# One product for both halves of the input, with the two sums added on leaving PSUM, in the input projections of an encoder layer

## The chip, the cores and the metric

The kernel runs on one core of a Trainium2 chip. The metric is the device time of one execution in microseconds, the median of the runs.

## The reference, cut to what matters

One encoder layer on 256 tokens of width 1024, all in float32. A combined input projection of the normalised stream feeds eight heads of forgetting attention and eight heads of a gated linear recurrence (HGRN2), and gives sigmoid merge gates. Both branches are projected, gated, summed and projected once more; a layer norm follows, then a mixture of sixteen experts of which each token uses two.

```python
x = layer_norm(x, ln_in_g, ln_in_b)
h = x @ w_in[l] + b_in[l]
fq, fk, fv, ff, hq, hf, hi, hg, gates = split_cols(h, IN_SIZES)
...
f_gate = lb + (1.0 - lb) * jax.nn.sigmoid(z)          # z: heads of hf
q_h = jax.nn.silu(to_heads(hq, HGRN_HEADS))
...
g = jax.nn.sigmoid(gates)
mixed = (g[..., :D_MODEL] * y_fox + g[..., D_MODEL:] * y_hgrn) @ w_mix_out[l] + b_mix_out[l]
x = layer_norm(ALPHA * x + mixed, ln1_g[l], ln1_b[l])
y_moe = grouped_top2_moe(x, router_w, router_b, expert_w1[l], expert_w3[l], expert_w2[l])
```

## The kernel before, in words

Float32 precision is kept with products of a rounded type (fp32r): each operand is split into a high half (the value rounded) and a low half (what is left), and a product of two operands is made of three: high by high, high by low, low by high, all summed in PSUM.

The **front stage** does everything before the experts. Its weights come as 15 slots of 128 x 4096 floats, each cut into 8 units of 512 columns; `u` counts the units, 0 to 119. `KIND` says how a slot is multiplied. In a token-major slot ("tm": 0, 3, 6, 13, 14) the input is the stationary operand and 512 weight columns move. In a feature-major slot ("fm": 1, 2, 4, 5, 7 to 10) a weight block of 128 x 128 is stationary and the input moves, all 256 tokens; one output block of 128 features needs two units, and a slot has four blocks. Slots 11 and 12 ("f4") are feature-major too, with the outputs of the branches as the input. The eight "fm" slots are: 1 the forget gate of the recurrence (`ev_hf`), 2 its query (`ev_hq`), 4 the attention's query (`ev_q`), 5 its key (`ev_k`), 7 to 10 the merge gates (`ev_gate`).

`prep(u)` splits the weights of a unit: ACT casts them to the high half (three units have their cast on DVE), and DVE, or POOL for some units, subtracts to get the low half. High and low halves have four buffers each, so the halves of unit u can be made when the products of unit u - 4 are done. `mm(u)` issues the products of a unit, in a feature-major slot four steps of three products (L215, L216, L217). When a block is complete, its `evac` function takes it out of PSUM in the next round, with the bias and the gate's nonlinearity. PSUM tiles with the tag "g" have four banks.

The order on PE, ACT, DVE and POOL is written out by hand: each engine does its instructions in the order in which the program gives them. A round `i` of the main loop is: what `pe` has for the round; the split of unit 2i + 3; the products of unit 2i; the evacuation of the blocks that were complete; what `post` has for the round; the split of unit 2i + 4; what `mid` has; the products of unit 2i + 1. Through `post`, DVE gets the residual operations (`resid`, L337 to L344) in rounds 5 to 14, the small operations of the attention's forget gates (`f_log`, round 6, and `f_log2`, round 12), and from round 13 on the recurrence: `h_exps` and `h_mul` prepare its operands on DVE and ACT, `h_scores`, `h_mask` and `h_out` work them off, and `h_range1` to `h_range3` (rounds 20 and 21) look for the smallest decay, with a transpose on PE (L610) that waits for a reduction on DVE (L606). In round 12 `h_ln` takes logarithms on ACT, with a table load. Attention runs in rounds 29 to 40 beside the merge gates' slots.

The **expert stage** follows. Its weights (16 experts of three matrices) stream through buffers that the front stage and the experts before leave; all transfers are issued on one queue (SP), in a fixed order. An output of 256 x 1024 is written at the end.

Of the kernel before, what the change touches and what calls it, by code (L numbers as in the profile page):

```python
# [18 lines left out]
T, D, NE, S = 256, 1024, 16, 64  # L19
# [44 lines left out]
def trunk(ctx: ExitStack, tc: tile.TileContext, x, cst_d, rows_d, wf, we, lvl_d, out):  # L64
    nc = tc.nc
    V, A, G, PE = nc.vector, nc.scalar, nc.gpsimd, nc.tensor
# [22 lines left out]
    def bank(tag, shape, name=None):  # L89

        return ps.tile(shape, F32, name=name or tag, tag=tag, bufs={"g": 4, "s": 2, "o": 2}[tag])
# [27 lines left out]
    def C(name):  # L119
        a, b = _C[name]  # L120
        return cst[:, a:b]
# [42 lines left out]
    KIND = ["tm", "fm", "fm", "tm", "fm", "fm", "tm", "fm", "fm", "fm", "fm", "f4", "f4", "tm", "tm"]  # L164
# [20 lines left out]
    tmp = {}  # L185
    evac = {}
    done = []

    def mm(u, tts=(0, 1)):
        i, c = u // 8, u % 8  # L190
        hi, lo = split[u]
        rh, rl = operands[i]()
        if KIND[i] == "tm":
            for tt in tts:
                if c == 0:

                    tmp[tt] = ([(bank("g", [128, 256]), 0), (bank("o", [128, 256]), 256)] if i == 14 and tt == 1
                               else [(bank("g", [128, 512]), 0)])
                t = slice(tt * 128, (tt + 1) * 128)
                for p, a in tmp[tt]:  # L200
                    b = a + 512 // len(tmp[tt])
                    PE.matmul(p, rh(c)[:, t], hi[:, a:b], start=c == 0, stop=False, skip_group_check=True)  # L202
                    PE.matmul(p, rh(c)[:, t], lo[:, a:b], start=False, stop=False, skip_group_check=True)  # L203
                    PE.matmul(p, rl(c)[:, t], hi[:, a:b], start=False, stop=c == 7, skip_group_check=True)  # L204
                if c == 7:
                    done.append((i, tt, [p for p, _ in tmp[tt]]))
            return
        nk = 8 if KIND[i] == "fm" else 4
        k0 = 4 * (c % 2) if nk == 8 else 0
        if k0 == 0:  # L210
            tmp["p"] = bank("g", [128, T])
        p = tmp["p"]
        for kk in range(4):
            k, w = k0 + kk, slice(kk * 128, (kk + 1) * 128)
            PE.matmul(p, hi[:, w], rh(k), start=k == 0, stop=False)  # L215
            PE.matmul(p, hi[:, w], rl(k), start=False, stop=False)  # L216
            PE.matmul(p, lo[:, w], rh(k), start=False, stop=k == nk - 1)  # L217
        if k0 + 4 == nk:
            done.append((i, c // 2 if nk == 8 else c, p))


    def halves(name):

        t = [X.tile([128, 2, 2, T], F32R, name=name, tag="w", bufs=4) for _ in range(4)]
        return [lambda k, i=i: t[k // 2][:, i, k % 2, :] for i in range(2)], t

    xp, xt4 = halves("xp")
# [20 lines left out]
    def x_affine(tt, j):  # L248
        p = xq[tt, j]
        if j == 0:  # L250
            xq["t", tt] = P2.tile([128, 8, 128], F32, name="xt", tag="hk" if tt else "lf")
        xt = xq["t", tt][:, 2 * j:2 * j + 2, :]
        for i in range(2):
            k = slice(2 * j + i, 2 * j + i + 1)
            if j % 2 == 0:
                V.tensor_scalar(xt[:, i, :], p[:, i, :], C("ing")[:, k], C("inb")[:, k], op0=OP.mult, op1=OP.add)
            else:
                A.activation(xt[:, i, :], p[:, i, :], AF.Identity, bias=C("inb")[:, k], scale=C("ing")[:, k])
        xq[tt, j] = xt

    def x_hi(tt, j):
        A.copy(xt4[j][:, 0, :, tt * 128:(tt + 1) * 128], xq[tt, j])

    def x_lo(tt, j):
        t = slice(tt * 128, (tt + 1) * 128)
        (G if j == 3 or (tt, j) == (1, 1) else V).tensor_sub(xt4[j][:, 1, :, t], xq[tt, j],
                                                             xt4[j][:, 0, :, t].bitcast(F32))

    operands = {i: (lambda: xp) for i in range(11)}
    def x_parts(tt, j):  # L270
        x_affine(tt, j)
        x_hi(tt, j)
        x_lo(tt, j)
# [17 lines left out]
    prep(0)  # L291
    prep(1)
    mm(0, (0,))
    x_stats(1)
    V.bn_aggr(mvs(1), sm[:, 24:36])
    mm(1, (0,))
    A.activation(mvs(1)[:, 1:2], mvs(1)[:, 1:2], AF.Sqrt, bias=eps_in[:, 0:1])
    prep(2)
# [4 lines left out]
    x_turn(1, 0)  # L303
    x_turn(1, 1)
    mm(2, (0,))
    mm(3, (0,))
    x_affine(1, 0)
# [18 lines left out]
    mm(3, (1,))  # L326
    prep(5)
    x_parts(0, 3)
    prep(6)
    x_parts(1, 3)  # L330
    prep(7)

# [50 lines left out]
    def p4(dt=F32, shape=(128, 4, T)):  # L383
        return P1.tile(list(shape), dt, name="p4", tag="p4")

    hv = GP.tile([128, 2, 512], F32, name="hv")
    lf = P2.tile([128, 4, T], F32, name="lf")
    hk = P2.tile([128, 4, T], F32, name="hk")
    hqt = P2.tile([128, 4, T], F32, name="hqt")
    qT = p4()  # L390
    kT = p4()
    vt = PB.tile([128, 2, 512], F32, name="vt")
    late = {}
# [374 lines left out]
    def ev_gate(n):  # L768
        def ev(b, p):
            i = 4 * n + b  # L770
            A.activation(late["gates"][:, i, :], p, AF.Sigmoid if i >= NID else AF.Identity, bias=C("bg")[:, i:i + 1])
        return ev
# [83 lines left out]
                 13: lambda tt, p: (mix_add(0, tt, p), mix_stats(0, tt))})  # L856
    for n in range(4):
        evac[7 + n] = ev_gate(n)
    operands[11] = lambda: [lambda k, i=i: oH[i][:, k, :] for i in "hl"]
    operands[12] = lambda: [lambda k, i=i: oF[i][:, k, :] for i in "hl"]  # L860
    operands[13] = operands[14] = lambda: late["mp"]
# [389 lines left out]
    pm, w, s1, s2, n1 = [t16[:, i] for i in range(5)]  # L1251
# [52 lines left out]
    def gather(g):  # L1304
        p = bank("g", [128, 4, 128])
        for i in range(4):
            k = 4 * g + i
            for tt in range(2):
                PE.matmul(p[:, i, :], raw[:, tt, k * 128:(k + 1) * 128], oneh2[:, tt, :], start=tt == 0, stop=tt == 1)  # L1309
        return p  # L1310
# [34 lines left out]
    def turn_pe():  # L1345
        p = bank("g", [128, 4, 128])
        for i in range(4):
            PE.transpose(p[:, i, :], sg[:, i * 128:(i + 1) * 128], ident)  # L1348
        return p
# [180 lines left out]
    for e in range(0, NE, 2):  # L1530
# [25 lines left out]
        p = turn_pe()  # L1556
# [11 lines left out]
        if e < LAST:  # L1568
            p = gather(0)
# [3 lines left out]
        if e < LAST:  # L1573
            py[0], py[1] = [bank("g", [128, 512]) for _ in range(2)]
            down(e, 0)
            p = gather(1)
# [132 lines left out]
```

## Time and profile before

| | |
|---|---|
| median of 3 runs | 676.27 us (676.14 to 677.37) |
| the profiled execution, its own time | 677.44 us |
| its span, first to last instruction | 675.7 us |
| PE busy | 650.1 us (96%) |
| PE weight loads (PEld) busy | 386.8 us (57%) |
| DVE, ACT, POOL busy | 210.1, 195.6, 75.9 us |
| mean granted clock of PE | 0.988 |

Times are microseconds from the span's start. PE stands for the matmul engine, PEld for its weight loads, which overlap the products; DVE, ACT, POOL and SP are the vector, scalar, general and transfer-issuing engines. An engine counts as busy while an instruction of it is on record. Products are pipelined and their ends are modelled, so the pace of PE is read from start to start. L215 is line 215 of the kernel before. "[0.76 <-ACT hqt L407]" behind an instruction means that its engine sat idle for 0.76 us before it, until ACT's instruction of line 407 on the tile `hqt` had ended. A granted clock of 1.00 is 2.4 GHz, 0.50 is 1.2 GHz.

### The profile page before, as it was taken

The page shows a single profiled execution, that of the slowest core. Times are in us where ns is not written, and L with a number is a line of the kernel's source. Part 1 is how long each engine was busy: PE and PEld are TensorE (multiplying, and loading weights), DVE is VectorE, ACT ScalarE, POOL GpSimd, SP SyncE. Part 2 cuts the span into 40 slices and gives each one's busy share as a digit, 9 for nine tenths or more (in the row PEclk, how much of TensorE's full clock was granted, in tenths as well). Part 3 has the DMA queues.
Part 4 walks back from the last instruction along what each step waited for, and adds up shares of the span by engine and source line. Part 5 has one row for each costly group of instructions (what it writes and reads, how often), then busy time and mean ns, then how long its engine had stood idle before and what let it go on. Part 6 is the DMA issues. An engine that isn't in the chain of part 4 may idle for free.

```text
span 675.7 us, 9394 instructions
## 1 busy us (share of the span) xinstructions
PE 650.1 (96%) x3773; PEld 386.8 (57%) x3773; DVE 210.1 (31%) x472; ACT 195.6 (29%) x413; POOL 75.9 (11%) x74
## 2 busy tenths in 40 slices
PE   7999999999999999999999999959999999799996
PEld 7796998999998734435444533513443443343542
DVE  6788855554585511011011011000101101101014
ACT  4664466767455410121111111101011011001211
POOL 1203365232272000000000000000000000000001
PEclk8999999999999999999999999979999999989999
DMA  8959325636888799999999999999999999999992
GB/s 325 412 212 368 138 82 211 249 125 238 316 306 346 268 348 400 420 431 418 430 421 419 431 418 430 421 419 426 422 421 429 420 428 423 420 428 422 414 374 101
DMA packets 31444, 238.70 MB, mean 353 GB/s; under 512 B 3488, under 2 KB 3616, under 8 KB 20640
## 3 DMA queue, kind: packets, MB, share of 16 engines
q1 hardware_dynamic: 31248, 237.94, 86.7%
q8 instruction: 32, 0.52, 0.3%
q14 instruction: 20, 0.16, 0.1%
q10 hardware_dynamic: 144, 0.07, 0.0%
HBM read 236.95 MB, written 1.05 MB: 352 GB/s over the span
## 4 chain that ended last, share of the span: by engine, by line
PE 57%; DMA 23%; DVE 2%; POOL 1%; ACT 1%; issue 0%; DVEq 0%; ACTq 0%; SPq 0%; POOLq 0%
DMA w<-in_we_dram 23%; PE g L1340 21%; PE g L1357 9%; PE g L215 4%; PE g L216 3%; PE g L217 3%; PE g L1309 2%; PE g L1385 2%; PE acc L1374 1%; PE g L203 1%; PE g L1510 1%; PE g L204 1%; PE g L202 1%; PE g L1348 1%; PE g L1499 1%; PE g L1406 1%
## 5 line engine op out<-in xcount | busy, mean ns | idle before, releaser
L1340 PE MATMUL g<-w,e 128*64 128x512 f32 x992 | 223.0, 600 | 7.3 <-DMA w<-in_we_dram 7.3
L1340 PEld LDWEIGHTS g<-w,e 128*64 128x64 f32 x992 | 69.4, 138 | 139.5 <-issue 127.4
L1357 PE MATMUL g<-w,f 128*64 128x512 f32 x448 | 106.4, 604 | 2.9 <-DMA w<-in_we_dram 2.9
L182 DVE TENSOR_TENSOR lo<-w,hi 128x512 fp32r<-128x512 f32 x87 | 67.7, 789 | 49.3 <-ACT hi L181 48.4
L181 ACT CAST hi<-w 128x512 fp32r<-128x512 f32 x117 | 70.2, 618 | 38.9 <-PE g L216 31.5
L1357 PEld LDWEIGHTS g<-w,f 128*64 128x64 f32 x448 | 41.4, 138 | 57.5 <-issue 53.4
L215 PE MATMUL g<-xp,hi 128*128 128x256 f32 x256 | 74.3, 290 | 0.0
L217 PE MATMUL g<-xp,lo 128*128 128x256 f32 x256 | 72.5, 283 | 0.2 <-DVE lo L182 0.2
L216 PE MATMUL g<-xp,hi 128*128 128x256 f32 x256 | 72.4, 283 | 0.0
L182 POOL TENSOR_TENSOR lo<-w,hi 128x512 fp32r<-128x512 f32 x33 | 45.2, 1372 | 111.8 <-ACT hi L181 111.8
L1369 DVE SCALAR_TENSOR_TENSOR y<-g,sm,y 128x512 fp32r<-128x512 f32 x14 | 10.5, 751 | 142.5 <-ACT y L1368 142.5
L1619 POOL TENSOR_TENSOR e<-e,par 128x256 f32<-128x256 f32 x2 | 1.4, 726 | 448.9 <-ACT e L1618 448.9
L215 PEld LDWEIGHTS g<-xp,hi 128*128 128x128 f32 x256 | 48.9, 191 | 2.6 <-issue 1.4
L217 PEld LDWEIGHTS g<-xp,lo 128*128 128x128 f32 x256 | 49.0, 191 | 0.4 <-DVE lo L182 0.4
L216 PEld LDWEIGHTS g<-xp,hi 128*128 128x128 f32 x256 | 49.0, 191 | 0.0
L1309 PEld LDWEIGHTS g<-e,raw 128*128 128x128 f32 x224 | 26.1, 192 | 11.4 <-issue 11.4
L1320 ACT ACTIVATE e<-g,cst 128x128 f32<-128x128 f32 x28 | 10.5, 456 | 69.0 <-PE g L1309 69.0
L1563 DVE TENSOR_TENSOR e<-e,g 128x512 f32<-128x512 f32 x8 | 5.5, 687 | 76.2 <-ACT e L1562 76.2
L1309 PE MATMUL g<-e,raw 128*128 128x128 f32 x224 | 28.7, 282 | 0.0
L1368 ACT ACTIVATE y<-g,sm 128x512 fp32r<-128x512 f32 x14 | 9.6, 687 | 61.2 <-PE g L1357 28.4
L1572 ACT COPY f<-g 128x512 f32<-128x512 f32 x8 | 4.7, 585 | 69.6 <-PE g L1348 69.6
L1549 DVE TENSOR_TENSOR e<-e,g 128x512 f32<-128x512 f32 x8 | 5.5, 687 | 47.9 <-PE g L1340 47.9
(325 smaller groups left out, 756.9 us busy)
## 6 DMA issues: line engine op xcount, KB each, us to landing
w<-in_we_dram SPq DMA_DIRECT2D x70, 2048.0 KB, 24.6
w<-in_we_dram SPq DMA_DIRECT2D x94, 512.0 KB, 18.5
w<-in_wf_dram SPq DMA_DIRECT2D x13, 2048.0 KB, 8.8
w<-in_wf_dram SPq DMA_DIRECT2D x8, 512.0 KB, 9.5
w<-in_we_dram SPq DMA_DIRECT2D x16, 256.0 KB, 5.2
rbc<-in_rows_dram SPq DMA_DIRECT2D x1, 1036.0 KB, 13.6
f<-in_we_dram SPq DMA_DIRECT2D x4, 256.0 KB, 7.3
out_dram<-par SPq DMA_DIRECT2D x4, 256.0 KB, 2.1
```

Source lines behind the costliest of these rows:

```text
L181: A.copy(hi, src)
L182: (G if on_pool(u) else V).tensor_sub(lo, src, hi.bitcast(F32))
L215: PE.matmul(p, hi[:, w], rh(k), start=k == 0, stop=False)
L216: PE.matmul(p, hi[:, w], rl(k), start=False, stop=False)
L217: PE.matmul(p, lo[:, w], rh(k), start=False, stop=k == nk - 1)
L1309: PE.matmul(p[:, i, :], raw[:, tt, k * 128:(k + 1) * 128], oneh2[:, tt, :], start=tt == 0, stop=tt == 1)
L1320: A.activation(t[:, i, :], p[:, i, :], AF.Identity, bias=C("b1")[:, 4 + i:5 + i], scale=C("g1")[:, 4 + i:5 + i])
L1340: PE.matmul(h[64 * nh:64 * nh + 64, :], xg[kh][:, k, 64 * (e % 2):64 * (e % 2) + 64], wcol(e, m + kh, k, nh), start=kh + k == 0, stop=kh = ...
L1357: PE.matmul(py[nh][64 * a:64 * a + 64, :], hT[a][:, c0:c0 + 64], wt[:, nh * 512:nh * 512 + 512], start=f == 0, stop=f == 7)
L1368: A.activation(y["h"], py[nh], AF.Identity, scale=gs)
L1369: V.scalar_tensor_tensor(y["l"], py[nh], gs, y["h"].bitcast(F32), op0=OP.mult, op1=OP.subtract)
L1385: PE.matmul(W["y"][64 * a:64 * a + 64, :], hT[a][:, c0:c0 + 64], w[:, 0:q], start=f == 0, stop=f == 7)
```

## The change

In the "fm" slots the high half of a weight block meets the high and the low half of the input in one product: the input's halves lie in one tile (`xt4`), 256 columns of each are taken as 512 moving columns, and the sum goes to the two halves of a full PSUM bank. The product of the weights' low half with the input's high half is added to the first of them. A step thus has one product of 512 columns and one of 256. In the last step of a block the low half's product comes first. When the block leaves PSUM, ACT copies the second sum into the place where the block's result will lie, DVE adds it to the first in PSUM, and the evacuation goes on as before from the first. Slots 11 and 12 keep three products of 256, in a like order.

```diff
@@ -208,13 +208,22 @@
         nk = 8 if KIND[i] == "fm" else 4
         k0 = 4 * (c % 2) if nk == 8 else 0
         if k0 == 0:
-            tmp["p"] = bank("g", [128, T])
-        p = tmp["p"]
+            tmp["p"] = bank("g", [128, 2, T])
+        p, side = tmp["p"], i in both
         for kk in range(4):
             k, w = k0 + kk, slice(kk * 128, (kk + 1) * 128)
-            PE.matmul(p, hi[:, w], rh(k), start=k == 0, stop=False)
-            PE.matmul(p, hi[:, w], rl(k), start=False, stop=False)
-            PE.matmul(p, lo[:, w], rh(k), start=False, stop=k == nk - 1)
+            last = k == nk - 1
+            if side:
+
+                both_mm = lambda: PE.matmul(p, hi[:, w], both[i](k), start=k == 0, stop=last, skip_group_check=True)
+            else:
+                both_mm = lambda: [PE.matmul(p[:, 0, :], hi[:, w], r(k), start=k == 0 and r is rh, stop=last and r is rl,
+                                             skip_group_check=True) for r in (rh, rl)]
+            if not last:
+                both_mm()
+            PE.matmul(p[:, 0, :], lo[:, w], rh(k), start=False, stop=False, skip_group_check=True)
+            if last:
+                both_mm()
         if k0 + 4 == nk:
             done.append((i, c // 2 if nk == 8 else c, p))
 
@@ -267,6 +276,7 @@
                                                              xt4[j][:, 0, :, t].bitcast(F32))
 
     operands = {i: (lambda: xp) for i in range(11)}
+    both = {i: (lambda k: xt4[k // 2][:, :, k % 2, :]) for i in range(11)}
     def x_parts(tt, j):
         x_affine(tt, j)
         x_hi(tt, j)
@@ -856,6 +866,23 @@
                  13: lambda tt, p: (mix_add(0, tt, p), mix_stats(0, tt))})
     for n in range(4):
         evac[7 + n] = ev_gate(n)
+
+    home_of = {1: lambda b: lf[:, b, :], 2: lambda b: hqt[:, b, :], 4: lambda b: qT[:, b, :], 5: lambda b: kT[:, b, :]}
+
+    def side_by_side(i, fn, to):
+        def ev(b, p):
+            if i in both:
+                t = to(b)
+                A.copy(t, p[:, 1, :])
+                V.tensor_add(p[:, 0, :], p[:, 0, :], t)
+            fn(b, p[:, 0, :])
+        return ev
+
+    for n in range(4):
+        home_of[7 + n] = lambda b, n=n: late["gates"][:, 4 * n + b, :]
+    for n in range(13):
+        if KIND[n] != "tm":
+            evac[n] = side_by_side(n, evac[n], home_of.get(n))
     operands[11] = lambda: [lambda k, i=i: oH[i][:, k, :] for i in "hl"]
     operands[12] = lambda: [lambda k, i=i: oF[i][:, k, :] for i in "hl"]
     operands[13] = operands[14] = lambda: late["mp"]
```

## Rows read from the trace of the kernel before

**Rows 1.** Page: span, busy time of the engines, DMA share in 40 slices.

```profile
span 675.7 us, 9394 instructions
...
PE 650.1 (96%) x3773; PEld 386.8 (57%) x3773; DVE 210.1 (31%) x472; ACT 195.6 (29%) x413; POOL 75.9 (11%) x74
...
DMA  8959325636888799999999999999999999999992
```

**Rows 2.** Windows: length, busy us (count) PE, PEld, DVE, ACT, POOL; clock, DMA share, GB/s.

```profile
31.10:52.60 21.50, 21.50 (x175) 21.32 (x176) 18.11 (x39) 13.15 (x29) 1.64 (x2) 1.00 0.64 248
...
66.70:88.60 21.90, 21.27 (x190) 19.90 (x186) 17.98 (x54) 10.32 (x26) 7.03 (x5) 1.00 0.39 154
88.60:113.20 24.60, 24.45 (x165) 21.68 (x166) 11.06 (x17) 15.97 (x29) 13.89 (x11) 1.00 0.32 114
113.20:162.60 49.40, 49.40 (x419) 46.02 (x418) 28.59 (x92) 36.46 (x88) 17.75 (x17) 1.00 0.53 199
162.60:174.30 11.70, 11.70 (x101) 11.65 (x98) 4.93 (x8) 6.23 (x12) 2.57 (x2) 1.00 0.90 333
...
230.00:235.00 5.00, 5.00 (x37) 3.50 (x36) 0.73 (x2) 1.23 (x4) 0.00 (x0) 1.00 0.30 54
...
260.00:280.00 20.00, 20.00 (x106) 10.36 (x104) 2.07 (x3) 2.09 (x5) 0.00 (x0) 1.00 1.02 427
```

**Rows 3.** Timeline of PE: products three apart, of 512 and of 256 columns.

```profile
62.07 0.39 PE L202 MATMUL g<-hi,xp 128*128 128x512 f32 x1
...
62.76 0.39 PE L202 MATMUL g<-hi,xp 128*128 128x512 f32 x1
...
171.02 0.28 PE L215 MATMUL g<-xp,hi 128*128 128x256 f32 x1
...
171.38 0.28 PE L215 MATMUL g<-xp,hi 128*128 128x256 f32 x1
```

**Rows 4.** Timeline of ACT, DVE and PE around the end of slot 2.

```profile
45.80 0.62 ACT L181 CAST hi<-w 128x512 fp32r<-128x512 f32 x1 [0.82 <-PE g L216]
...
52.09 0.47 ACT L407 ACTIVATE hqt<-g,cst 128x256 f32<-128x256 f32 x1
...
52.59 0.48 DVE L408 SCALAR_TENSOR_TENSOR hqt<-g,cst,hqt 128x256 f32<-128x256 f32 x1 [0.76 <-ACT hqt L407]
...
55.35 0.17 DVE L692 TENSOR_TENSOR ff<-ff 128x16 f32<-128x16 f32 x1 [1.17 <-ACT ff L690]
...
58.03 0.50 PE L203 MATMUL g<-lo,xp 128*128 128x512 f32 x1 [0.69 <-DVE lo L182]
```

**Rows 5.** Lines by form: copy and add of 128x256 from PSUM, busy us, mean ns.

```profile
L715 ACT COPY nf<-g 128x256 f32<-128x256 f32 x4 | 1.5, 372 | 5.0 <-DVE nf L714 3.4 <-PE g L217 1.6
...
L782 DVE TENSOR_TENSOR gates<-g,gates 128x256 f32<-128x256 f32 x8 | 3.0, 416 | 0.0
```

**Rows 6.** Waits of DVE, 31.1 to 52.6 us: total us, times, longest.

```profile
DVE hqt L408 <- ACT hqt L407: 1.7, 2, 1.0
DVE lo L182 <- ACT hi L181: 1.4, 4, 0.5
```

**Rows 7.** Timeline of DVE and PE at the search for the smallest decay.

```profile
88.36 0.16 DVE L606 TENSOR_REDUCE hrg<-hrg 128x1 f32<-128x16 f32 x1
...
88.57 0.27 PE L610 MATMUL g<-cst,hrg 128*1 128x128 f32 x1 [0.63 <-DVE hrg L606]
```

**Rows 8.** Windows of line L217 alone: length, busy us (count) PE, PEld; clock, DMA.

```profile
88.60:101.00 12.40, 6.80 (x24) 4.59 (x24) 1.00 0.17 52
113.20:162.60 49.40, 27.10 (x96) 18.32 (x96) 1.00 0.53 199
162.60:174.30 11.70, 8.93 (x32) 6.14 (x32) 1.00 0.90 333
```

**Rows 9.** Windows around the longest wait of the expert stage, columns as in rows 2.

```profile
444.00:451.00 7.00, 0.57 (x5) 0.17 (x5) 0.00 (x0) 0.00 (x0) 0.00 (x0) 0.81 0.97 401
451.00:458.00 7.00, 7.00 (x24) 2.35 (x26) 0.00 (x0) 0.00 (x0) 0.00 (x0) 0.70 1.05 428
```

## Prediction

> **What bounds the kernel now.** I read the page first. PE is busy 96% of a span of 675.7 us and the DMA engines are full from about a third of the span on [rows 1], so one of the two sets the end everywhere. The windows by stage come next. From 260 us on, in the expert stage, the queues run without a pause; but at 230 to 235 us the DMA share is 0.30 [rows 2]: the transfers wait there for buffers that PE has not yet left. So whatever moves the moment at which the front stage (projections, attention, recurrence, mixing) ends moves the start of the saturated stretch by the same amount, and with it the end. The change lies wholly in the front stage, and I count front-stage time one to one.
>
> Inside the front stage PE is at its floor nearly everywhere (21.50 of 21.50, 49.40 of 49.40, 11.70 of 11.70 us busy [rows 2]). The floor itself is read from start to start, since ends are modelled: three products of 256 columns start 0.36 us apart in all, and three of 512 columns 0.69 us [rows 3], thus 0.120 and 0.230 us each. The weight load of the next product lies beside it.
>
> But two engines stand close behind PE. DVE is busy 18.11 of 21.50 us in the stretch of the first two feature-major slots and 17.98 of 21.90 us in the stretch of the recurrence [rows 2]. And at the seam between these stretches PE already waits for DVE: the product at 58.03 us starts late for a low half [rows 4], which means that there the weight halves are ready with no lead at all. Going back from it: the low half follows a cast on DVE, behind three small operations of which the first waited 1.17 us for a logarithm on ACT, behind the Ln table and the last sigmoid of slot 2 at 52.09 us [rows 4]. Elsewhere the halves come early: ACT's cast at 45.80 us waits for PE to leave a buffer [rows 4], with four buffers per half.
>
> **What the change removes.** In each of 256 steps (8 slots of 8 units of 4) the products of 256 columns go from three to one plus one of 512. One weight load goes too. The columns are the same, so only the per-product overhead is won: 0.360 before, 0.230 + 0.120 = 0.350 after, 0.010 us a step, if the doubled product with its two separate runs of 256 elements takes what a plain one takes (bounds: 0, if it costs two of 0.120; 0.013, if both shapes go at the best spacing in the traced stretches). All 256 steps give 2.6 us, and only where PE sets the pace.
>
> The Trainium skill speaks of the same saving: "TensorE: Matmul & The Clock Gate", section "Back-to-back issue gap", gives 262 cycles for 256 columns and 518 for 512, so the saving would be 6 cycles, 2.5 ns a step or 0.6 us in all. At 2.4 GHz 256 columns are 107 ns, so the rows show some 13 ns of overhead on a short product, more than the page has; the rows decide.
>
> **What it adds.** 32 blocks (8 slots of 4) each get a copy on ACT, priced by the nearest PSUM copy of the same shape at 372 ns, and an add on DVE, by a PSUM operation of the same shape at 416 ns [rows 5] (bounds 0.37, the copy's time, and 0.48, the PSUM operation at 52.59 us [rows 4]; no row writes PSUM from DVE). More weighs the order. Before, a block's first activation stands on ACT right behind the cast, and DVE comes to its result later. Now ACT copies, DVE adds behind the low half that precedes it in its queue, ACT's activation waits for the add, and DVE's next operation on the block waits for the activation. Behind the waiting activation stands the next weight cast; behind the waiting DVE operation stand a residual operation and the next low half.
>
> *Slots 1 and 2 (8 blocks, 31 to 52.6 us).* When DVE is the pacer, a block makes its chain longer by the add 0.42, the sigmoid 0.47, and two hand-offs of 0.03 (52.09 + 0.47 to 52.59 [rows 4]): 0.95 us. Eight make 7.6 us. DVE has 21.50 - 18.11 = 3.4 us idle there to set against it [rows 2]; 3.1 of that are waits on ACT's casts and sigmoids [rows 6], which vanish when DVE runs behind. One, about 0.2, stays, because a cast follows a sigmoid that itself waits for DVE. So the last sigmoid of slot 2, and with it the whole chain to the low half at 58 us, comes 7.6 - 3.4 + 0.2 = 4.4 us later. The lead of the halves (a cast can start when the unit four before is done, so some three units of 1.44 us less 1.3 us for cast and subtraction, 3.0 us) covers PE up to slot 2's end, but at 58 us the lead is nil, so PE takes the 4.4 us there in full. Bounds: 0 if the queues overlap so that only the adds' own 8 x 0.42 = 3.4 us count against the 3.4 idle; 5.5 if the add costs 0.48 and each block has a second hand-off.
>
> *Slot 4 (4 blocks, 66.7 to 88.6 us).* The stretch is a chain of DVE and ACT, and it ends where PE waits for the smallest decay, DVE's operation at 88.36 us [rows 7]. Four adds lie ahead of it: 4 x 0.42 = 1.7 us. The copies are hidden, as ACT has 10.32 of 21.90 us busy [rows 2]. The consumer of this slot is a DVE operation, so no hand-off back to ACT. Bounds 0 and 2.5 (each add also waits 0.2 for its copy).
>
> *Slots 5 and 7 to 10 (20 blocks).* Here PE is the pacer and ACT and DVE are 11 to 16 of 25 and 36 and 29 of 49 us busy [rows 2]. Twenty copies and stalls of ACT for the add (about 0.8 us each) fall into idle time; the halves lead by some 3 us, as above, so I cost them at nothing; without that cover up to 0.8 us for a block, some 3 us for the four blocks with a softmax round beside them. PE's gain counts in these: 24 + 96 + 32 = 152 steps [rows 8] x 0.010 = 1.5 us won (bounds 0 and 2.0).
>
> **The sum.** +4.4 + 1.7 - 1.5 = +4.6 us. The profiled execution took 677.44 us (span 675.7 and 1.7 around it), so 682.0; that execution lies 1.17 above the median of the runs shown, 676.27, so the forecast for the median is 680.9 us, 0.7% slower.
>
> **Rivals.** *A: DVE never becomes the pacer, and the change is faster.* If casts and adds interleave so that the eight blocks' lag at 52.6 us stays within idle time and the one at 88 us too, then all 256 steps count: 676.27 - 2.6 = 673.7 us. For it: the 3.0 us of lead and 3.4 us of idle. Against it: PE's wait at 58.03 us has no lead, and the order on each engine is fixed. It decides when the chain of eight blocks grows by under 0.43 us each (3.4 / 8). Chance 0.13.
>
> *B: partly absorbed.* Half of the lag (2.2) and half of slot 4 (0.8) against 2.0 won: +1.0, 677.3 us, within what can be told. Chance 0.10.
>
> *C: more is lost.* A stall of over 4 us at 58 us may bring the granted clock down: after PE's near idleness from 444 to 451 us (0.57 of 7.00 busy) it was 0.70 over the next seven [rows 9], so about 0.3 x 7 = 2.1 us of PE's work, and the softmax stretch may add 1 to 3. 684 to 686 us. Against it: PE has slack of waits behind 58 us anyway. Chance 0.08.
>
> *D: the doubled product takes twice 0.120*, so that nothing is won: +6.1, 682.4 us. It does then not do what it says. The plain product of 512 columns in rows 3 speaks against it. Chance 0.05.
>
> *E: the weight loads set PE's pace.* PEld is busy 11.65 of 11.70 us at 162.6 to 174.3 [rows 2]. If a load had to take its 0.120 us turn and the columns were free, two loads a step instead of three would save 256 x 0.120 = 31 us: 645 us. Against it: 512 columns start 0.230 apart with the same loads, so columns, not loads, pace. Chance 0.02. The rule behind it is the Trainium skill's "Perfetto Trace Analysis", section "Identifying the Most-Contended Engine": TensorE's headroom is judged by how busy LDWEIGHTS is. Here it misleads, as load records overlap their wait.
>
> **How the numbers follow.** The forecast itself has 0.62 (its own range 678.3 to 682.8). Slower by over 0.2% (1.35 us, about what a measurement of this kernel can tell from no change): forecast, C and D, 0.75. Within: B, 0.10. Faster: A and E, 0.15. The range leaves out most of A and E below and the upper part of C: 675.0 to 684.5 us.
>
> **What would show it.** Right: L217's partner of 512 columns 0.23 us from the next start; DVE's waits on casts gone between 31 and 52 us, and in their place DVE and ACT waiting for each other at the block's add and activation; the Ln table load some 4 us later than 52.58; PE's wait for the low half, now ending at 58.03, ending near 62; the wait for the decay at 88 us near 94; no new PE waits after 113; the first expert product about 4.6 us later, the expert stage as long as before. Wrong: if the Ln table load moves by under 1.5 us, the step of the eight blocks fails (A or B); if PE's steps do not shrink to 0.350, the removal fails (D); if new PE waits show at 120 to 160 us, "at nothing" fails (C); if the front is late but the end is not, the one-to-one step fails.

## The result, and the profile after

The changed kernel took 686.02 us (median of 4 runs, 684.32 to 686.96) against 676.62 us of the kernel before in the same session (4 runs, 676.14 to 677.37): a ratio of 1.0129, interval 1.0114 to 1.0144. The forecast of slower was right; the size was not: 9.4 us where 4.6 were forecast, and above the upper end of the range, 684.5. The profiled execution took 684.32 us, 6.88 more than the profiled one of before.

The page (the DMA row is its share in 40 slices):

```profile
span 682.5 us, 8911 instructions
...
PE 652.2 (96%) x3517; PEld 373.3 (55%) x3517; DVE 220.1 (32%) x504; ACT 204.4 (30%) x445; POOL 76.8 (11%) x74
...
DMA  8976325733978889999999999999999999999992
```

Against [rows 1] PE has 256 products and loads fewer (3773 to 3517), DVE and ACT have 32 instructions more each, and PE's busy time did not fall. The windows by stage, moved along with the work (columns as in [rows 2]):

```profile
31.00:52.50 21.50, 20.76 (x114) 16.68 (x113) 17.87 (x40) 12.61 (x30) 0.51 (x1) 1.00 0.77 281
...
71.30:93.20 21.90, 19.93 (x141) 16.80 (x141) 17.74 (x52) 11.23 (x30) 6.95 (x5) 1.00 0.35 132
93.20:117.80 24.60, 24.45 (x142) 20.57 (x143) 13.01 (x22) 17.23 (x33) 14.13 (x11) 1.00 0.33 116
117.80:169.60 51.80, 49.69 (x322) 40.84 (x321) 31.22 (x101) 38.61 (x96) 17.53 (x16) 1.00 0.52 190
...
236.90:241.90 5.00, 5.00 (x37) 3.50 (x36) 0.73 (x2) 1.27 (x4) 0.00 (x0) 1.00 0.27 72
267.00:287.00 20.00, 20.00 (x106) 10.38 (x104) 2.07 (x3) 2.09 (x5) 0.00 (x0) 1.00 1.02 427
```

Two stretches in which PE was busy without a gap in [rows 2] now have gaps: 20.76 of 21.50 us at slots 1 and 2, and 49.69 of 51.80 at the merge gates with the softmax. The recurrence's stretch has 19.93 of 21.90. The last two rows show the seam to the experts and the saturated stretch as they were in [rows 2], only some 7 us later.

The waits of PE in the front stage, 24 to 235 us (total us, times, longest):

```profile
PE g L620 <- DVE hrg L616: 2.0, 1, 2.0
PE g L202 <- DVE hi L179: 1.6, 1, 1.6
PE g L203 <- DVE lo L182: 1.4, 2, 1.2
PE g L218 <- ACT gates L781: 1.1, 1, 1.1
PE o L600 <- ACT pts L762: 1.0, 2, 0.6
PE g L224 <- DVE lo L182: 0.9, 3, 0.3
```

Line numbers moved: L610 and L606 of before are L620 and L616, L215 to L217 are now L218 (512 columns) and L224 (the low half, 256), the copy and the add are L876 and L877. The wait for the decay was 0.63 [rows 7], the one for a low half 0.69 [rows 4]. The rows of L218 and L600 have no counterpart: of the kernel before, the profile lists no wait of PE between 100 and 200 us. Of the three waits in the last row two are new as well, 0.34 us at 46.10 and 0.32 us at 49.48: in slot 2 PE already waits for low halves, and the lead of the halves did not last to that slot's end.

Where the time came in is read by following the same instruction through the traces: the last low-half product of a unit, the product at the decay search, the first product of the experts' part (the gather), the span's end. Shifts are in us against the first trace of before; the last column is the median less that of before in the same session.

| kernel | slot 1, first unit | slot 4, first unit | decay | slot 7, first unit | slot 7, third unit | slot 10, first unit | gather | end | median |
|---|---|---|---|---|---|---|---|---|---|
| before, at us | 28.35 | 68.17 | 88.57 | 114.56 | 119.22 | 164.06 | 229.50 | 675.66 | |
| changed | -0.49 | +3.55 | +4.60 | +4.36 | +5.61 | +6.98 | +6.86 | +6.89 | +9.40 |
| changed_again | -0.38 | +4.85 | +4.73 | +4.50 | +5.76 | +7.12 | +6.99 | +7.21 | +8.17 |
| before_again | -0.25 | -0.26 | -0.25 | -0.22 | -0.22 | -0.22 | -0.22 | +0.65 | +0.10 |
| products_alone | -0.66 | -1.05 | -1.03 | -1.27 | -1.33 | -1.94 | -2.07 | -0.80 | -0.71 |
| evacuation_alone | -0.03 | +3.99 | +5.02 | +5.02 | +6.34 | +7.93 | +8.04 | +8.65 | +9.07 |
| slots_1_2 | +0.16 | +4.07 | +4.08 | +5.36 | +5.36 | +5.35 | +5.45 | +4.15 | +4.49 |
| slots_4_5 | -0.51 | -0.40 | +0.78 | +2.06 | +2.05 | +2.04 | +2.12 | +1.38 | +3.22 |
| slots_7_10 | -0.26 | -0.15 | -0.13 | -0.16 | +1.10 | +2.44 | +2.35 | +3.19 | +2.47 |
| activation_later | -0.42 | +0.01 | +0.58 | +0.33 | +1.71 | +1.68 | +1.83 | +1.70 | +2.50 |
| gates_sum_in_sbuf | +0.69 | +0.80 | +0.82 | +0.81 | +1.55 | +0.97 | +0.85 | +0.07 | +0.08 |
| sums_rearranged | +0.85 | +1.34 | +1.35 | +1.11 | +1.86 | +1.60 | +1.48 | +0.93 | +0.66 |

The first column is reached before the change has done much: it scatters from 0.66 us below to 0.85 above, in the same program by 0.25, so a shift is best read less its first column. For the changed kernel that is 6.86 + 0.49 = 7.35 at the gather: 4.04 up to slot 4, 1.05 from there to the decay, -0.24 in slot 5 and the token-major slot behind it, 2.50 from slot 7 on (7.35 - 4.85). The cut at slot 4 is not a firm one: in changed_again PE is 5.23 late there and 5.11 at the decay. The two kernels with parts of the change give the shares up to the decay better, 3.92 (slots_1_2) and 1.29 (slots_4_5).

**Slots 1 and 2.** The timeline of the last blocks of slot 2 and of what hangs on them:

```profile
51.91 0.69 DVE L182 TENSOR_TENSOR lo<-w,hi 128x512 fp32r<-128x512 f32 x1
...
52.52 0.42 DVE L877 TENSOR_TENSOR g<-g,hqt 128x256 f32<-128x256 f32 x1
...
52.98 0.47 ACT L417 ACTIVATE hqt<-g,cst 128x256 f32<-128x256 f32 x1 [0.79 <-DVE g L877]
...
53.48 0.48 DVE L418 SCALAR_TENSOR_TENSOR hqt<-g,cst,hqt 128x256 f32<-128x256 f32 x1 [0.54 <-ACT hqt L417]
...
56.04 1.28 ACT L536 ACT_TABLE_LOAD   x1
...
59.79 0.49 PE L202 MATMUL g<-hi,xp 128*128 128x512 f32 x1 [1.63 <-DVE hi L179]
...
61.46 0.50 PE L203 MATMUL g<-lo,xp 128*128 128x512 f32 x1 [1.18 <-DVE lo L182]
```

DVE's add stands behind its low half; ACT idles 0.79 us for the add; DVE idles 0.54 us for ACT's activation (0.47 and the hand-offs); then the next round. Before, the table load for the logarithms stood here:

```profile
52.58 1.28 ACT L526 ACT_TABLE_LOAD   x1
```

Now it comes at 56.04 instead of 52.58, 3.46 later, and PE's waits at the seam end at 61.46 instead of 58.03 [rows 4], 3.43 later. The waits from 31 to 57 us, DVE's and then ACT's (total us, times, longest):

```profile
DVE hqt L418 <- ACT hqt L417: 2.2, 4, 0.5
DVE lf L413 <- ACT lf L411: 1.6, 3, 0.5
DVE lf L413 <- issue: 0.6, 1, 0.6
DVE lo L182 <- ACT hi L181: 0.2, 1, 0.2
...
ACT lf L411 <- DVE g L877: 4.9, 4, 1.7
ACT hqt L417 <- DVE g L877: 4.5, 4, 1.6
```

Of the waits for casts in [rows 6] (1.4 us) one of 0.2 is left, and each block has one wait of DVE for ACT and one of ACT for DVE.

**Slots 7 to 10.** The timeline at the three places where PE lost time there:

```profile
121.61 0.37 ACT L876 COPY gates<-g 128x256 f32<-128x256 f32 x1
...
121.74 0.79 DVE L182 TENSOR_TENSOR lo<-w,hi 128x512 fp32r<-128x512 f32 x1 [0.91 <-ACT hi L181]
...
122.45 0.42 DVE L877 TENSOR_TENSOR g<-g,gates 128x256 f32<-128x256 f32 x1
122.90 0.47 ACT L781 ACTIVATE gates<-g,cst 128x256 f32<-128x256 f32 x1 [0.93 <-DVE g L877]
...
123.43 0.50 PE L218 MATMUL g<-xp,hi 128*128 128x512 f32 x1 [1.08 <-ACT gates L781]
...
141.29 0.48 ACT L781 ACTIVATE gates<-g,cst 128x256 f32<-128x256 f32 x1 [0.91 <-DVE g L877]
...
142.27 0.87 ACT L762 COPY pts<-s 128x384 f32<-128x384 f32 x2
...
142.81 0.81 PE L600 MATMUL o<-pts,vt 128*64 128x256 f32 x3 [0.45 <-ACT pts L762]
...
167.58 0.47 ACT L781 ACTIVATE gates<-g,cst 128x256 f32<-128x256 f32 x1 [1.48 <-DVE g L877]
167.95 0.85 ACT L762 COPY pts<-s 128x384 f32<-128x384 f32 x2
168.47 0.81 PE L600 MATMUL o<-pts,vt 128*64 128x256 f32 x3 [0.58 <-ACT pts L762]
```

At 123.43 PE needs a bank of PSUM, which the block still holds: it is copied, waits for the add behind a low half, and for the activation behind the add. At 142.81 and 168.47 PE needs the transposed probabilities (`f_probs`, L762), whose copies stand on ACT behind an activation that waited 0.91 and 1.48 us for its add. The shift of the changed trace, read from start to start, rises by 1.25, 0.86 and 0.98 us at these places, 3.1 together; the waits that the profile lists there, counted from the modelled ends, are 1.08, 0.45 and 0.58.

### The profile page after: what moved, and what is told of

It reads as the page before. It is cut to its first block, busy times and chain, and to the rows that moved or that the text cites. A ratio compares the mean times of both kernels' runs of the same rounds, so it can differ in the third digit from the quotient of the medians.

```text
span 682.5 us, 8911 instructions
## 1 busy us (share of the span) xinstructions
PE 652.2 (96%) x3517; PEld 373.3 (55%) x3517; DVE 220.1 (32%) x504; ACT 204.4 (30%) x445; POOL 76.8 (11%) x74
## 3 DMA queue, kind: packets, MB, share of 16 engines
HBM read 236.95 MB, written 1.05 MB: 349 GB/s over the span
## 5 line engine op out<-in xcount | busy, mean ns | idle before, releaser
L218 PE MATMUL g<-xp,hi 128*128 128x512 f32 x256 | 93.3, 404 | 1.1 <-ACT gates L781 1.1
L224 PE MATMUL g<-xp,lo 128*128 128x256 f32 x256 | 67.0, 282 | 1.0 <-DVE lo L182 0.9
L218 PEld LDWEIGHTS g<-xp,hi 128*128 128x128 f32 x256 | 47.3, 188 | 12.3 <-issue 1.7
L224 PEld LDWEIGHTS g<-xp,lo 128*128 128x128 f32 x256 | 48.3, 189 | 4.5 <-DVE lo L182 2.6
L1590 DVE TENSOR_TENSOR e<-e,g 128x512 f32<-128x512 f32 x8 | 5.5, 687 | 76.2 <-ACT e L1589 76.2
L202 PE MATMUL g<-hi,xp 128*128 128x512 f32 x48 | 20.0, 416 | 2.0 <-DVE hi L179 1.6
L203 PE MATMUL g<-lo,xp 128*128 128x512 f32 x48 | 20.1, 419 | 1.8 <-DVE lo L182 1.4
L220 PE MATMUL g<-p,hi 128*128 128x256 f32 x128 | 21.6, 279 | 0.0
```

Source lines behind the costliest of these rows:

```text
L218: both_mm = lambda: PE.matmul(p, hi[:, w], both[i](k), start=k == 0, stop=last, skip_group_check=True)
L220: both_mm = lambda: [PE.matmul(p[:, 0, :], hi[:, w], r(k), start=k == 0 and r is rh, stop=last and r is rl, skip_group_check=True) for r i ...
L224: PE.matmul(p[:, 0, :], lo[:, w], rh(k), start=False, stop=False, skip_group_check=True)
```

## The experiments

The kernel before was measured again in each session: 677.07, 677.14 and 677.15 us. The sums themselves cost what was expected; by form (busy us, mean ns) in the changed kernel:

```profile
L877 DVE TENSOR_TENSOR g<-g,gates 128x256 f32<-128x256 f32 x16 | 6.9, 429 | 1.5 <-ACT gates L876 1.0
L876 ACT COPY gates<-g 128x256 f32<-128x256 f32 x16 | 6.0, 372 | 0.0
```

**Products alone.** The doubled product without copy and add: the second sum (high halves of the weights by low halves of the input) is left out.

```diff
-            if i in both:
-                t = to(b)
-                A.copy(t, p[:, 1, :])
-                V.tensor_add(p[:, 0, :], p[:, 0, :], t)
```

> Leaves out the copy and the add, so the second sum (weights' high half by input's low half) never enters the result: the products are those of the change, the evacuation is that of before. Theory Q (the queues' order at the evacuation makes the loss; the products win 0.35 us less per unit of 10 steps): about 2.2 us faster than before (64 units by 0.035 us, the rate at which the shift shrinks from unit to unit in the changed kernel's trace), and PE's waits before 60 us as before. Rival P (the doubled product with its two runs and its full bank is itself the loss): same or slower than before.

676.36 us, ratio 0.9986 (0.9976 to 0.9995). The gather comes 1.4 us earlier, less the first column, where 2.2 were expected, and the median is 0.7 lower: the steps shrink, but by less than 0.010 us each (1.41 us over 256 steps is 5.5 ns).

**Evacuation alone.** Three products of 256 columns as before, into the two halves of the bank, with copy and add. Each half is opened by a product of its own, and what comes out is not the right sum; this variant is read for its time alone.

```diff
-                both_mm = lambda: PE.matmul(p, hi[:, w], both[i](k), start=k == 0, ...)
+                both_mm = lambda: [PE.matmul(p[:, n, :], hi[:, w], r(k), start=k == 0, ...)
+                                   for n, r in ((0, rh), (1, rl))]
```

> Three products of 256 columns as before, but high by low goes to the second half of the bank, and copy and add stay: the evacuation of the change without its doubled product. Theory Q: slower than before by the whole loss of the change and by the 1.3 us that its shorter steps win back behind 88 us, so +10 to +11 us. Rival P: within 1 us of before.

686.14 us, 1.0132 (1.0114 to 1.0150), +9.1 where +10 to +11 were expected: the whole loss, without the new product. In the trace the gather is 8.07 later, and with the 1.4 of the products taken off that is 6.7, near the changed kernel's 7.35.

**The change by slots.** Only the slots named are changed.

```diff
-    both = {i: (lambda k: xt4[k // 2][:, :, k % 2, :]) for i in range(11)}
+    both = {i: (lambda k: xt4[k // 2][:, :, k % 2, :]) for i in (1, 2)}
```

> The change in slots 1 and 2 alone; the other six feature-major slots as before. Theory Q (the eight blocks' chain of DVE and ACT): Ln table load some 4 us late, PE's wait for the low half of unit 28 and first product of slot 4 3.6 us late as in the changed kernel's trace, and then nothing more: +3.6 us at the end. Rival W (only the adds' own work counts, 8 by 0.42, set against 3.4 us of idle time): under +0.5 us. If the clock that falls in the long wait costs more than is hidden, +4.5 to +6.

681.56 us, 1.0065 (1.0051 to 1.0080). Slot 4 starts 3.9 later, less the first column, as in the whole change. That nothing more would come did not hold: PE's trace has one more gap, 1.11 us at 111.56 ahead of a token-major product (L204), for which the profile shows no cause; before's trace has none there.

With (4, 5) in that place:

> The change in slots 4 and 5 alone. By the changed kernel's trace 1.3 us at the search for the smallest decay, against 16 units by 0.035 won, of which only the six behind it count, 0.2: +1.1 us. By the prediction's term (four adds of 0.42) +1.5 us. If the two other parts (slots 1 and 2 +4.4, slots 7 to 10 +2.2) add up with this one to the whole 9.4, +2.5 us.

680.36 us, 1.0049 (1.0035 to 1.0063): +3.2, more than each of the three expected sizes. The decay comes 1.29 later, less the first column; another 1.28 come behind it in slot 5, where the whole change lost nothing. The windows before, in and behind them show why (columns as in [rows 2]):

```profile
86.90:89.40 2.50, 0.47 (x5) 0.16 (x3) 2.40 (x9) 1.60 (x3) 0.50 (x1) 1.00 0.00 0
89.40:93.60 4.20, 4.20 (x17) 3.63 (x18) 2.04 (x4) 3.20 (x8) 3.19 (x3) 0.59 0.00 0
93.60:98.00 4.40, 4.40 (x41) 3.67 (x39) 2.14 (x4) 2.19 (x6) 4.32 (x4) 1.00 0.01 4
```

PE waited, and the granted clock over the next 4.2 us was 0.59, near the lower level of 1.2 GHz. The steps of slot 5 start 0.64 us apart there, where 0.355 is usual:

```profile
90.26 0.63 PE L218 MATMUL g<-xp,hi 128*128 128x512 f32 x1
...
90.90 0.63 PE L218 MATMUL g<-xp,hi 128*128 128x512 f32 x1
```

So slot 5 lost by the clock, not by its own copies and adds.

With range(7, 11):

> The change in the merge gates' slots alone. By the changed kernel's trace: three waits of PE (1.2 for a bank that an activation still reads, 0.9 and 1.0 for the probabilities' copies that stand on ACT behind a waiting activation), 3.1 us, against 32 units by 0.035 us won, 1.1: +2.0 us. The prediction's own step (costed at nothing, hidden by lead): 1.1 to 1.3 us faster than before.

679.54 us, 1.0033 (1.0021 to 1.0045). The 2.5 us come in at the same three places as in the whole change (+1.26 at slot 7's third unit, the rest at units 68 and 80), with the same waits of PE, 1.1 for a gate's activation and 1.1 for the probabilities' copies. What was costed at nothing is here by itself: +2.0 had been expected from the trace, 1.1 to 1.3 faster by the prediction's own step.

**The activation later.** All slots changed, but a block's first reader is given to its engine behind the next split of weights; the sums are all there.

```diff
-            fn(b, p[:, 0, :])
+                later.append(lambda: fn(b, p[:, 0, :]))
...
         prep(2 * i + 4)
+        finish()
```

> The change, with the activation of each block (and DVE's operations behind it) issued after the round's second weight split instead of right behind the add; in round 12, where the tables change, as in the change. Same instructions, same work, another order on ACT and DVE. Theory Q (waits in the queues make the loss): DVE no longer waits for the sigmoid, so a block lengthens its chain by the add's 0.35 to 0.42 us alone; eight of them go into the 3.4 us of idle time. About 3 us of slots 1 and 2 come back and one to three of slots 7 to 10: +3 to +5 us against before. Rival W (the added work itself): +8 to +9.5 us as in the change.

679.64 us, 1.0034 (1.0022 to 1.0047): some 6 of the 8 to 9 us are gone with no work removed, more than expected. The end of slot 2 on ACT in this kernel:

```profile
50.77 0.62 ACT L181 CAST hi<-w 128x512 fp32r<-128x512 f32 x1 [0.53 <-PE g L218]
...
52.16 0.47 ACT L417 ACTIVATE hqt<-g,cst 128x256 f32<-128x256 f32 x1 [0.50 <-DVE g L877]
...
52.65 1.28 ACT L536 ACT_TABLE_LOAD   x1
```

The cast waits for PE again, as at 45.80 in [rows 4], and the table load stands at 52.65. Slot 4 starts 0.43 later, less the first column, instead of 4.04. What stays is 1.0 at the decay and a wait of 1.3 for a bank at slot 7; of the waits for the probabilities one of 0.2 is left (PE, 24 to 235 us):

```profile
PE g L218 <- DVE p L661: 1.3, 1, 1.3
...
PE o L600 <- ACT pts L762: 0.2, 1, 0.2
```

From slot 7's third unit to the gather the shift grows by 0.12, in the changed kernel by 1.25.

**The gates' sum in SBUF.** Slots 7 to 10 alone: ACT adds the bias to the second sum on its way to SBUF, DVE adds the first sum there, and the sigmoids of the last gates are taken in bulk in rounds 42 and 44. DVE's add waits for ACT, but nothing on ACT waits for DVE's add.

```diff
-            A.activation(late["gates"][:, i, :], p, AF.Sigmoid if i >= NID else AF.Identity, ...)
+            g = late["gates"][:, i, :]
+            A.activation(g, p[:, 1, :], AF.Identity, bias=C("bg")[:, i:i + 1])
+            V.tensor_add(g, p[:, 0, :], g)
```

> The change in slots 7 to 10 alone, but ACT adds the bias to the second sum on its way out, DVE adds the first sum to it in SBUF, and the sigmoid comes for several blocks at once two rounds later: nothing on ACT waits for DVE's add, and the bank is free at the add. Theory Q (ACT's wait and the bank held for it cost slots 7 to 10 their 3.1 us): the waits at units 58 and at the probabilities are gone, and 32 units by 0.035 us are won: the front stage 0.8 to 1.3 us earlier than before, the end 0 to 1.3 earlier. Rival W (16 added operations on each of ACT and DVE): still +1.5 to +2.5 us.

677.22 us, 1.0000 (0.9991 to 1.0009). The waits of PE from 113 to 235 us:

```profile
PE g L218 <- DVE gates L783: 0.6, 1, 0.6
PE g L1301 <- DVE sel L1298: 0.5, 1, 0.5
PE g L203 <- DVE lo L182: 0.2, 1, 0.2
```

The wait for the probabilities is gone, that for the bank is halved, and with it goes the loss of these slots: the gather is 0.16 later, less the first column, instead of 2.61. The front did not come 0.8 to 1.3 us earlier, as theory Q had it, since half of the bank's wait stays. All sixteen adds are there; ACT has somewhat less to do, as the copy takes in the bias and seven sigmoids go in bulk. That the waits for the probabilities come from the order and not from ACT's work is shown by the activation later, where every instruction stayed.

**The change once more, and the kernel before once more.** To see what repeats.

> The change itself once more, for a second trace. Its first trace has the front stage 6.86 us late and the end 6.89 us late, but its runs lie 9.4 us above those of before at the median. Theory: the front stage is late by 6.5 to 7 us each time (it is set by fixed orders), and the rest, 1 to 3 us, comes and goes in waits that no queue explains or in the expert stage. Rival: the front stage itself is 9 us late in most executions, and the first trace was an easy one.

685.31 us (684.19 to 687.02), 1.0125 (1.0108 to 1.0143). From the decay to the gather its trace lies within 0.15 us of the first one. Up to there it differs: slot 4 starts 1.3 later. The windows from 60 to 68 us, of the first trace and of this one (columns as in [rows 2]):

```profile
60.00:68.00 8.00, 6.82 (x23) 5.20 (x23) 7.86 (x14) 3.05 (x7) 3.82 (x3) 0.79 0.31 109
```

```profile
60.00:68.00 8.00, 6.83 (x17) 5.15 (x18) 7.86 (x16) 3.15 (x7) 3.12 (x3) 0.57 0.31 107
```

Behind the same waits (1.6 and 1.2 us) the granted clock was 0.79 in one and 0.57 in the other, and the decay came at the same time in both: DVE, 7.86 of 8.00 us busy, sets the pace there, not PE.

> The kernel before, unaltered, to see how far one trace and one median of the same program can lie from another. If the 1.5 to 2.5 us that the changed kernel's median lost beyond what its trace shows at the first gather are only the scatter of single executions and traces, this run's median and its milestones in the trace will differ from the other run of the same program by up to 1 us. If they agree within 0.3 us, those 1.5 to 2.5 us belong to the changed kernel.

677.25 us, 1.0003 (0.9994 to 1.0012). The milestones of the front lie within 0.04 us of the first trace of before, once the 0.25 of the start are taken off; the expert stage took 0.87 longer (0.65 + 0.22). The medians agree within 0.1 us, so by the words above what the changed kernel's medians lose beyond its traces is its own.

**All sums rearranged.** Slots 1 and 2 as in the activation later, slots 5 and 7 to 10 with the sum in SBUF, slot 4 as before.

```diff
+    both = {... for i in (1, 2, 5, 7, 8, 9, 10)}
...
-        A.activation(kT[:, b, :], p, AF.Identity, bias=C("bk")[:, b:b + 1])
+        A.activation(kT[:, b, :], p[:, 1, :], AF.Identity, bias=C("bk")[:, b:b + 1])
+        V.tensor_add(kT[:, b, :], p[:, 0, :], kT[:, b, :])
```

> The change in slots 1, 2, 5 and 7 to 10, with all its sums rearranged; slot 4, where the add stands on the chain of VectorE itself, is left as before. Slots 1 and 2: copy and add as in the change, but the block's first activation stands behind the next weight casts. Slots 5 and 7 to 10: ScalarE adds the bias to the second sum on its way to SBUF, VectorE adds the first sum there, and the sigmoids of the last gates are taken in bulk later. Theory one (what was lost is the order in the queues, and the sums themselves are nearly free): the front's gather within 1 us of before's, no wait of TensorE for a bank over 0.8 us in slots 7 to 10, and a time from 0.8 us under to 1.0 us over before's. Theory two (the copies and adds themselves cost engine time that comes to the end): the 28 remaining adds and copies leave at least half of the change's loss, 3 us or more over before.

677.81 us, 1.0006 (0.9995 to 1.0017). The gather is 0.63 later, less the first column; 0.75 comes in at slot 7 (1.11 to 1.86), where PE waits for the bank. Theory one holds: 28 of the 32 adds are there, and the loss is not. Of the copies only the eight of slots 1 and 2 are left as they were; in the other slots the copy takes in the bias. No version with all its sums beats the kernel before: what the products save is no more than what is left of the waits.

## Why the prediction was wrong in size

**The pace of the steps: right in kind, the term too large.** In the trace after, a step goes from L218 to L218:

```profile
140.79 0.40 PE L218 MATMUL g<-xp,hi 128*128 128x512 f32 x1
...
141.02 0.28 PE L224 MATMUL g<-xp,lo 128*128 128x256 f32 x1
...
141.14 0.40 PE L218 MATMUL g<-xp,hi 128*128 128x512 f32 x1
```

That is 0.23 and 0.12, and four steps from 140.08 on start 1.42 us apart in all, 0.355 a step. The shifts fall by 0.23, 0.19, 0.28 and 0.19 us over the stretches of slots 5 and 7 to 10 between PE's waits: 0.9 us won where 1.5 were forecast. Rivals D and E fall with it: the doubled product starts 0.23 to 0.24 us ahead of the next, as a plain one does, and products_alone wins 1.41 us where D has nothing; and with one load fewer a step is 5 to 6 ns shorter, not 120 as in E. The estimate of 2.5 ns a step from the Trainium skill ("TensorE: Matmul & The Clock Gate", section "Back-to-back issue gap") is nearer to the 5 to 6 ns here than the 10 forecast; the traces lie between.

**Slots 1 and 2: right, a little large.** +4.4 forecast; 4.04 in the changed kernel, 3.91 with these slots alone, 3.46 at the table load. The add took 0.42 and DVE's wait for the activation 0.54, where 0.95 in all had been put. That it is the order and not the work, the activation later shows. This is why rival A (the lag stays in idle time) fails. One detail was wrong without a price of its own: the lead of the halves did not cover PE up to slot 2's end (0.34 and 0.32 us of waits at 46 and 49 us).

**Slot 4: right, a little large.** +1.7 forecast, 1.05 in the whole, 1.29 with slots 4 and 5 alone. The two together put the decay at 93.18; "near 94" had been forecast.

**Slots 5 and 7 to 10: the step that failed.** "Twenty copies and stalls of ACT for the add (about 0.8 us each) fall into idle time; the halves lead by some 3 us, as above, so I cost them at nothing". The size of a stall was right in the mean (15 waits of ACT's gate activations for the add, 0.75 us each), and in these slots the halves were never late. But the lead of the halves covers only the halves. ACT's queue serves PE in two other ways that have no such lead: it frees the bank that the next block needs, and it copies the probabilities that PE's next product reads. They cost 1.25, 0.86 and 0.98 us, and the prediction's own sign for this, new waits of PE at 120 to 160 us, is what the trace shows. The prediction itself had a price for stalls without cover, "some 3 us for the four blocks with a softmax round beside them", and set it aside. Slots 7 to 10 alone lose 2.5 us of the median, and the sum in SBUF gives it back; with the activation later, and all the work in place, the waits for the probabilities nearly go. So for these two waits the order is shown to be the cause; for the bank it rests on the profile's releaser and on the wait being halved once the add frees the bank. For slot 5 the word "nothing" held: the whole change lost no time there. With 3.1 lost and 0.9 won where 0 and 1.5 stood, and slots 1, 2 and 4 at 5.09 for 6.1, the sum is 5.09 - 0.9 + 3.1 = 7.3, the 7.35 of the trace.

**One to one to the end: right in the traces.** 6.86 at the gather, 6.89 at the end. In single executions the expert stage varies by about 1 us either way (0.87 longer in the kernel before run again, 1.27 longer in products_alone, 1.3 shorter in slots_1_2), so a small gain or loss in the front can't be followed through it.

**Rival C** came nearest in time (684 to 686) and had "the softmax stretch may add 1 to 3", which is what happened. Its other half did not: the clock fell behind the stall at 58 us, but a clock of 0.57 there put the decay no later than one of 0.79 (5.11 and 5.09), since DVE set the pace behind it.

**What stays open.** The front lost 7.35 and 7.37 us in the two traces of the changed kernel, the medians 9.40 and 8.17. Both profiled executions were among the shorter of theirs (684.32 and 684.65 of eight from 684.19 to 687.02), and the profiled one of before was its longest, 677.44. Of the 9.40, 1.7 and 0.8 us are these two distances. This matters for the size: 7.35 above the median of before, 676.62, would be 684.0, within the range, and only the rest took the time out of it. Where the longer executions spend their 1 to 2 us was not in a trace. Their mean granted clock (0.982 to 0.989) does not set them apart from the three shorter ones (0.984 to 0.988), so the clock is not shown to be it. The gap of 1.11 us at 111.56 in slots_1_2 has no cause shown.

## What to carry to other kernels

When an evacuation is cut in two over two engines, ask not only whether the work fits into their idle time, but what stands behind each waiting instruction in its queue, and for each consumer of that queue (weight halves, PSUM banks, operands of the next product) what lead it has of its own. A sum that goes out and back (ACT, DVE, ACT, DVE) makes each block a chain; if the engine that starts also finishes its part in one instruction (bias on the way out, the nonlinearity later in bulk), nearly the same work cost next to nothing here (28 of the 32 adds, +0.66 us, not told from zero). A few nanoseconds a product were not worth a new dependence on each block.

## What was not expected of the hardware

The same idleness of PE was followed by different clocks: 0.47 of 2.50 us busy, then 0.59 granted, in slots_4_5; in the changed kernel at the same place 0.43 of 2.40 us busy, then 1.00 (windows 90.80 to 93.20 and 93.20 to 97.40 us). And the same waits at 58 us gave 0.79 in one execution and 0.57 in another of one program. A clock that falls behind a stall is thus no fixed price: it cost 1.28 us in slots_4_5 between the decay and slot 7, and behind the stall at 58 us the lower of two clocks left no mark at the decay, as PE wasn't the pacer there.
